# Making the residual stream channel-major in a three-pass encoder-layer kernel

## Chip, cores, metric

The kernel runs as one program on the 8 cores of one Trainium2 chip; each core handles half of one prompt stream and four short sample streams. The metric is device time in microseconds (us) of the slowest core. In some executions the cores of one die show a lower granted TensorE clock and the run is some per cent longer (up to 3032 us here, with 0.81 to 0.82 on one die and 0.985 to 0.986 on the other). Only fast runs are compared below, unless a median of all runs is said to include a slow one.

TensorE is called PE, VectorE DVE, ScalarE ACT, GpSimd POOL, as in the profile.

## The reference, cut to what matters

One layer on 8192 prompt frames x 4 streams and 16 frames x 32 sample streams, D = 1024, feed-forward width 2816 = 22 x 128:

```python
x = x + 0.5 * swiglu_ffn(x, g_ff1, w_ff1_in, w_ff1_out)       # pass A: "first FFN"
z = rms_norm(x, g_mix) @ w_in                                  # pass B: "mixer"
#   conv group: GLU -> depthwise conv (31) -> LayerNorm -> swish
#   attention group: 8 q / 2 kv heads, window of 3 chunks, sinks
x = x + concat([c_out, a_out]) @ w_out                         # "output product"
x = x + 0.5 * swiglu_ffn(x, g_ff2, w_ff2_in, w_ff2_out)       # pass C: "second FFN"

def swiglu_ffn(x, g, w_up, w_down):
    a, b = split(rms_norm(x, g) @ w_up)                        # "up product"
    return (silu(a) * b) @ w_down                              # "down product"
```

All three passes read the residual x from HBM and write it back.

## The kernel before

The cuts of code in this document are shortened: within a function too, lines are left out, and `# [...]` marks a longer gap.

The program records every operation and then orders each engine's instructions with a list scheduler on a cost model; the order is static, so PE takes its matmuls in that order and waits where one isn't ready. That is why nearly every instruction of the profile has one source line; groups are told apart by tile names. Tiles of the first FFN begin with `A_`, of the mixer with `B_`, of the second FFN with `C_`.

x is row-major: 128 frames on the partitions, 1024 channels along the free dimension. A norm then works on one number per partition (0.16 us an operation in the trace), but the up product contracts over channels, so every normed group of 128 rows goes through PE as eight transposes:

```python
def norm_vec(self, x, n, G):                 # x: [128 rows, 1024]
    O.act(out=b[0:n, :], in_=x[0:n, :], func=AF.Square, accum_out=ssq)
    rsqrt(O, ssq, 1.0 / D, v, y, t, u)       # Newton on [128, 1] operands
    O.stt(b[0:n, :], x[0:n, :], y, G[0:n, :], ALU.mult, ALU.mult)

def transposes(self, b, n):
    for k in range(8):
        self.O.tr(p[:, k * 128:k * 128 + n], b[0:n, k * 128:(k + 1) * 128], self.K.IDB[0:n, 0:n])

def up(self, bi, bg):                        # blocks of 384 columns (the first: 448 or 320)
    for j in range(NJ):
        for h, ps in ((0, a), (1, b)):
            for k in range(8):
                O.mm(ps[:, 0:N], W[:, k, h * 128:(h + 1) * 128], X[:, k, 0:N], k == 0, k == 7)
# [...]
def down(self, bi, bg):                      # rows stationary, w_down moving (512 wide)
    for gi, g in enumerate(self.blocks[bi]):
        for h in range(2):
            for j in range(NJ):
                O.mm(p[0:n, :], self.H[:, j, off:off + n], self.WD[:, j, h * 512:(h + 1) * 512], j == 0, j == NJ - 1)
            O.stt(x[0:n, h * 512:(h + 1) * 512], p[0:n, :], 0.5, x[0:n, h * 512:(h + 1) * 512], ALU.mult, ALU.add)
# [...]
def load_x1(self, r, n):                     # mixer: x comes back from HBM, ring of three tiles [128, 1024]
    i = self.nxt("x1", 3)
    self.O.dma("gpsimd", "bx1%d" % i, self.X1[i][0:n, :], self.d.x1[r:r + n, :], rk=[("x1", r)])

def out_pe(self, r, n, lhs, h):              # output product: mixer rows stationary, w_out moving
    for k in range(8):
        O.mm(p[0:n, :], lhs(k), self.WO[:, k, h * 512:(h + 1) * 512], k == 0, k == 7)

def out_post(self, r, n, h):
    self.O.tt(x[0:n, c], self.pb[1 - h][0:n, :], x[0:n, c], ALU.add)
    if h == 1:
        self.O.dma("gpsimd", "bx2%d" % i, self.d.x2[r:r + n, :], x[0:n, :], wk=[("x2", r)])
# [...]
def loads(F):                                # second FFN's weights, loaded while the mixer still runs
    for j in range(NJ):
        F.load_w(j)                          # w_up: 22 tiles, into memory that frees during the mixer
    for j in range(NJ):
        F.load_d(j)                          # w_down: into memory that frees at the mixer's end
```

Of the kernel before, what the change touches and what calls it, by code (L numbers as in the profile page):

```python
# [7 lines left out]
F32 = mybir.dt.float32  # L8
# [9 lines left out]
SLACK = 2  # L18
# [8 lines left out]
class Prog:  # L27
# [124 lines left out]
    def schedule(self, rounds=3):  # L152
# [18 lines left out]
        def run(before, after, prio, back):  # L171
# [24 lines left out]
            for _ in range(n):  # L196
# [9 lines left out]
                if dma[u] and not back:  # L206
                    pipe = max(pipe, end + 0.5) + wire[u]
                    end = max(pipe, end + 1.5) + 0.3 + SLACK
                dirty = {e}
                for x in after[u]:  # L210
                    left[x] -= 1
                    lat = 0.06 if eng[x] == e else 0.16 + (MARGIN if back else 0.0)
                    if back and dma[x]:
                        lat += 2.0 + SLACK + wire[x]
                    if ready[x] < end + lat:
                        ready[x] = end + lat
                    if not left[x]:
                        release(x)
                        dirty.add(eng[x])
# [220 lines left out]
HALO0 = HALF  # L440
SAMP0 = HALF + 128
NROWS = HALF + 192
# [5 lines left out]
def bcast_rows(ap1, n=128):  # L448
    return ap1.partition_broadcast(n)


class FF:
# [3 lines left out]
    def __init__(self, K, carves, tag, wu, wd, g1, g2, blocks, src, dst, xnd=None, rkey=None, wkey=None, nkey=None, low=None, cwd=None, weng="gpsimd", hook=None):  # L456
# [3 lines left out]
        self.rkey, self.wkey, self.nkey = rkey, wkey, nkey  # L460
        nmax = max(sum(n for _, n in b) for b in blocks)
        self.weng, self.hook = weng, hook
        c0, c1, c2 = carves
        self.XA = [c0([128, D], F32, "xa") for _ in range(2)]
        self.XB = [c0([128, D], BF16, "xb") for _ in range(2)]
        self.G1 = c0([128, D], F32, "g1")
        self.SM = c0([128, 8, 16], F32, "sm")
        self.XNT = [c0([128, 8, nmax], BF16, "xnt") for _ in range(2)]
        self.SA = [c0([128, nmax], F32, "sa") for _ in range(2)]
        self.nmax = nmax  # L470
        self.H = c0([128, NJ, nmax], BF16, "h")
        self.H_off = c0.off - (NJ * nmax * 2 + 63) // 64 * 64
# [3 lines left out]
        c3 = c0 if cwd is None else cwd  # L476
        self.WD = c3([128, NJ, 1024], BF16, "wd")
        self.XR = [c3([128, D], F32, "xr") for _ in range(3)]
        self.XO_off = c3.off
        self.XO = [c3([128, 8, 128], BF16, "xo") for _ in range(2)] if g2 is not None else None  # L480
        self.G2 = c3([128, D], F32, "g2") if g2 is not None else None
        self.cnt = dict(xa=0, xr=0, xb=0, xo=0, sm=0, ab=0, d=0, t=0)
        self.g1, self.g2 = g1, g2
# [3 lines left out]
        self.xa, self.xr = {}, {}  # L487

    def nxt(self, k, n):
        i = self.cnt[k]  # L490
        self.cnt[k] += 1
        return i % n

    def load_g(self, which):
        G, g = (self.G1, self.g1) if which == 1 else (self.G2, self.g2)
        if G is not None:
            self.O.dma("sync", self.tag + "g%d" % which, G[:, :], bcast_rows(g))

    def stage(self):

        O, P = self.O, self.K.P
        lo = self.XO_off
        ring = self.XR + [self.G2, P.sbuf(self.tag + "_sx", [128, D], F32, lo)]
        chunks = [(self.WU[j][:, h * 1024:(h + 1) * 1024], self.wu[j][:, h * 1024:(h + 1) * 1024]) for j in range(NJ) for h in range(2)]
        chunks += [(self.WD[:, j, :], self.wd[j]) for j in range(NJ)]
        for i, (dst, src) in enumerate(chunks):
            s = ring[i % len(ring)]
            O.dma("sync", self.tag + "sg%d" % (i % len(ring)), s[:, :], src)
            O.cp(dst, s[:, :])

    def first(self):

        O, P, off = self.O, self.K.P, self.H_off + 22 * self.nmax * 2 - 12288
        xs = self.XA + [P.sbuf(self.tag + "_xh%d" % i, [128, D], F32, off + 4096 * i) for i in range(2)]
        bs = self.XB + [P.sbuf(self.tag + "_bh%d" % i, [128, D], BF16, off + 8192 + 2048 * i) for i in range(2)]
        for i, (r, n) in enumerate(self.blocks[0]):
            O.dma("gpsimd" if i % 2 else "sync", self.tag + "xh%d" % i, xs[i][0:n, :], self.src[r:r + n, :])
        self.load_g(1)
        self.stage()
        sm = self.SM[:, :, :].rearrange("p a b -> p (a b)")  # L520
        O.memset(sm[:, 0:4], 1.0)
        for i, (r, n) in enumerate(self.blocks[0]):
            O.act(out=bs[i][0:n, :], in_=xs[i][0:n, :], func=AF.Square, accum_out=sm[0:n, i:i + 1])
        y = sm[:, 8:12]
        rsqrt(O, sm[:, 0:4], 1.0 / D, sm[:, 4:8], y, sm[:, 12:16], sm[:, 16:20])
        o = 0
        for i, (r, n) in enumerate(self.blocks[0]):
            O.stt(bs[i][0:n, :], xs[i][0:n, :], y[0:n, i:i + 1], self.G1[0:n, :], ALU.mult, ALU.mult)
            p = self.transposes(bs[i], n)
            O.act(out=self.XNT[0][:, :, o:o + n], in_=p, func=AF.Copy)  # L530
            o += n

    def load_w(self, j):
        k = [("pc", self.tag + "u", j)] if self.weng == "sync" else []
        self.O.dma(self.weng, self.tag + "wu%d" % (j % 8), self.WU[j][:, :], self.wu[j], rk=k)

    def load_d(self, j):
        k = [("pc", self.tag + "d", j)] if self.weng == "sync" else []
        self.O.dma(self.weng, self.tag + "wd%d" % (j % 8), self.WD[:, j, :], self.wd[j], rk=k)

    def load_xa(self, g):
        r, n = g
        i = self.nxt("xa", len(self.XA))
        self.xa[g] = self.XA[i]
        self.O.dma("sync", self.tag + "xa%d" % i, self.XA[i][0:n, :], self.src[r:r + n, :], rk=self.rkey(g) if self.rkey else ())

    def load_xr(self, g):
        r, n = g
        i = self.nxt("xr", len(self.XR))
        self.xr[g] = (self.XR[i], i)  # L550
        self.O.dma("sync", self.tag + "xr%d" % i, self.XR[i][0:n, :], self.src[r:r + n, :], rk=self.rkey(g) if self.rkey else ())

    def norm_vec(self, x, n, G):
        O = self.O
        b = self.XB[self.nxt("xb", 2)]
        sm = self.SM[:, self.nxt("sm", 8), :]
        ssq, v, y, t, u = (sm[0:n, i:i + 1] for i in range(5))
        O.act(out=b[0:n, :], in_=x[0:n, :], func=AF.Square, accum_out=ssq)
        rsqrt(O, ssq, 1.0 / D, v, y, t, u)
        O.stt(b[0:n, :], x[0:n, :], y, G[0:n, :], ALU.mult, ALU.mult)  # L560
        return b

    def transposes(self, b, n):
        p = self.PT[self.nxt("t", 2)][:, :].bitcast(BF16)
        with self.O.group():
            for k in range(8):
                self.O.tr(p[:, k * 128:k * 128 + n], b[0:n, k * 128:(k + 1) * 128], self.K.IDB[0:n, 0:n])
        return p.rearrange("p (k n) -> p k n", k=8)[:, :, 0:n]

    def norm1(self, bi):  # L570

        O = self.O
        X = self.XNT[bi % 2]
        off = 0
        prev = None
        for g in self.blocks[bi] + [None]:
            cur = None
            if g is not None:
                cur = (self.norm_vec(self.xa[g], g[1], self.G1), g[1], off)
                off += g[1]  # L580
            yield
            if prev is not None:
                b, n, o = prev
                p = self.transposes(b, n)
                O.act(out=X[:, :, o:o + n], in_=p, func=AF.Copy)
            prev = cur
            yield

    def tail(self, g):

        O = self.O
        (r, n) = g
        x, xi = self.xr[g]
        O.dma("gpsimd", self.tag + "st%d" % xi, self.dst[r:r + n, :], x[0:n, :], wk=self.wkey(g) if self.wkey else ())
        if self.G2 is None:
            return
        b = self.norm_vec(x, n, self.G2)
        yield
        yield
        p = self.transposes(b, n)  # L600
        i = self.nxt("xo", 2)
        O.act(out=self.XO[i][:, :, 0:n], in_=p, func=AF.Copy)
        O.dma("gpsimd", self.tag + "xo%d" % i, self.xnd(g), self.XO[i][:, :, 0:n], wk=self.nkey(g))
        yield

    def up(self, bi, bg):
        O = self.O
        N = sum(n for _, n in self.blocks[bi])
        X = self.XNT[bi % 2]
        for j in range(NJ):  # L610
# [13 lines left out]
            if j == 10:  # L624
                assert not self.pend
                for g in self.blocks[bi][0:3]:
                    self.load_xr(g)

    def run(self, prologue=None):
        self.pend = []  # L630
        norm = [None]

        def bg(k):
            for _ in range(k):
                while self.pend:
                    try:
                        next(self.pend[0])
                        return
                    except StopIteration:
                        self.pend.pop(0)  # L640
# [1005 lines left out]
```

## Time and profile before

2573 us, the median of four runs (one of them slow, at 2976; the mean of the three fast ones is 2572.8). The profiled run is a fast one; the slowest of its cores spans 2569.6 us.

I cut the span at PE events that can be read off the trace of each core, and take the median of the eight cores:

| stage | from / to | before, us | PE idle in it |
|---|---|---|---|
| start-up | start / end of the first down product | 148.4 | |
| first FFN | / its last down matmul | 883.8 | 0.6 |
| mixer | / the last output matmul | 598.7 | 53.5 |
| gap | / the second FFN's first down matmul | 34.1 | 11.2 |
| second FFN | / its last down matmul | 889.5 | |
| tail | / end | 9.2 | |

The mixer and the gap aren't mixer work alone: the up product of the second FFN's first block is woven into them.

The page of the kernel before: busy time of the engines, the busy tenths of PE and its granted clock in 40 slices of the span, and the chain of work that ended last.

```profile
PE 2463.4 (96%) x14740; PEld 1354.3 (53%) x14740; DVE 1063.0 (41%) x2748; ACT 748.8 (29%) x1307; POOL 202.4 (8%) x356
...
PE   6999999999999999899899969799999999999998
...
PEclk9999999999999999899999979999999999999999
...
PE 91%; DMA 4%; DVE 2%; issue 2%; ACT 1%; DVEq 0%; SPq 0%; POOL 0%; POOLq 0%; ACTq 0%
```

PE is the kernel's chain nearly everywhere. Slices 24 and 26 (about 1478 to 1540 and 1606 to 1670 us) are not full.

Windows of the same core: the stretch and its length, the busy time of PE, PEld (weight loads), DVE, ACT and POOL with instruction counts, then PE's granted clock, DMA's busy share, and GB/s.

```profile
300.00:364.00 64.00, 64.00 (x384) 35.35 (x383) 31.62 (x101) 18.53 (x31) 8.61 (x14) 1.00 0.42 117
1478.00:1542.00 64.00, 39.84 (x242) 22.86 (x242) 41.51 (x99) 33.79 (x48) 14.06 (x23) 0.76 0.84 261
1542.00:1606.00 64.00, 63.25 (x407) 38.23 (x405) 32.23 (x88) 17.63 (x30) 13.95 (x25) 1.00 0.71 231
1606.00:1670.00 64.00, 46.15 (x253) 24.59 (x250) 20.33 (x61) 10.39 (x18) 6.20 (x12) 0.90 0.77 251
1800.00:1864.00 64.00, 64.00 (x362) 34.90 (x360) 14.83 (x33) 9.32 (x18) 1.06 (x2) 1.00 0.12 38
```

In the steady FFN windows PE is busy 64 of 64 us and DVE less than half: what PE is given to do there is the time. At the mixer's end PE is idle for 24 of 64 and 18 of 64 us, with DMA at 0.84 and 0.77.

### The profile page before, as it was taken

To read this page: it belongs to the slowest core of one execution; us is meant where nothing else is said; L and a number is where in the kernel's file an instruction comes from. 1 tells how busy PE (TensorE), PEld (TensorE's weight loads), DVE (VectorE), ACT (ScalarE), POOL (GpSimd) and SP (SyncE) were. 2 spreads that over 40 slices of the span, in tenths; PEclk is the share of its full clock that TensorE was granted. 3 is DMA by queue.
4 is the path that set the end of the run, shared out by engine and by line. 5 is a ranking of instruction groups with operands and counts; after the bars stand their busy time and mean duration, and the time that the engine had idled before them with its cause. 6 is when DMAs were issued, how large, how long until landed. Compare 5 with 4: busy or idle time off the path is not lost.

```text
span 2569.6 us, 41607 instructions; the slowest of 8 cores (2559.8 to 2569.6 us)
## 1 busy us (share of the span) xinstructions
PE 2463.4 (96%) x14740; PEld 1354.3 (53%) x14740; DVE 1063.0 (41%) x2748; ACT 748.8 (29%) x1307; POOL 202.4 (8%) x356
## 2 busy tenths in 40 slices
PE   6999999999999999899899969799999999999998
PEld 3355555555556555455455535355555555555554
DVE  5454344335434432564876865321233223313211
ACT  3122232223213211465766652111121112112210
POOL 0011011011101000010111122000000000000000
PEclk9999999999999999899999979999999999999999
DMA  9965344344434433433355787721112111210110
GB/s 277 306 180 116 76 112 121 74 93 123 108 75 108 111 101 101 108 88 94 93 148 165 208 261 232 250 70 50 34 49 74 50 42 58 74 49 27 40 50 25
DMA packets 116867, 284.24 MB, mean 111 GB/s; under 512 B 33983, under 2 KB 51391, under 8 KB 115703
## 3 DMA queue, kind: packets, MB, share of 16 engines
q1 hardware_dynamic: 86359, 166.28, 21.8%
q0 software_dynamic: 30304, 115.29, 16.2%
q8 instruction: 121, 1.98, 0.3%
q14 instruction: 83, 0.68, 0.1%
HBM read 230.89 MB, written 97.86 MB: 128 GB/s over the span
## 4 chain that ended last, share of the span: by engine, by line
PE 91%; DMA 4%; DVE 2%; issue 2%; ACT 1%; DVEq 0%; SPq 0%; POOL 0%; POOLq 0%; ACTq 0%
PE PS L373 91%; DMA A_xr<-wu 1%; DMA C_xa<-x 1%; DMA B_x_159<-x 1%; ACT B_pt L373 0%; DMA A_xa<-xin 0%; DVE C_sm L373 0%; DMA A_xr<-wd 0%; DVE B_y L373 0%; DMA C_wu<-wu2b 0%; DMA B_x_158<-x 0%; DVE A_wu L373 0%; DVE A_xb L373 0%; DVE A_sm L373 0%; DVE B_x_158 L373 0%
## 5 line engine op out<-in xcount | busy, mean ns | idle before, releaser
L373 PE MATMUL PS<-A_xnt,A_wu 128*128 128x384 bf16 (+1 forms) x3872 | 652.7, 329 | 8.5 <-DVE A_wu L373 6.6
L373 PE MATMUL PS<-C_xnt,C_wu 128*128 128x384 bf16 (+1 forms) x3872 | 632.4, 325 | 7.3 <-DMA C_wu<-wu2b 6.4
L373 PEld LDWEIGHTS PS<-A_xnt,A_wu 128*128 128x128 bf16 x3872 | 376.1, 98 | 267.5 <-issue 17.4
L373 PEld LDWEIGHTS PS<-C_xnt,C_wu 128*128 128x128 bf16 x3872 | 379.8, 98 | 251.2 <-issue 8.3
L373 ACT ACTIVATE C_sa<-PS 128x384 f32<-128x384 f32 (+1 forms) x242 | 117.4, 485 | 759.0 <-PE PS L373 718.5
L373 PE MATMUL PS<-A_wd,A_h 128*128 128x512 bf16 x1496 | 331.1, 379 | 0.7 <-DVE A_h L373 0.7
L373 PE MATMUL PS<-C_wd,C_h 128*128 128x512 bf16 (+1 forms) x1452 | 317.3, 381 | 0.0
L373 DVE TENSOR_TENSOR C_h<-PS,C_sa 128x384 bf16<-128x384 f32 (+1 forms) x242 | 133.2, 551 | 374.5 <-PE PS L373 369.2
L373 DVE TENSOR_TENSOR A_h<-PS,A_sa 128x384 bf16<-128x384 f32 (+1 forms) x242 | 135.9, 562 | 285.5 <-PE PS L373 282.4
L373 PEld LDWEIGHTS PS<-A_wd,A_h 128*128 128x128 bf16 x1496 | 142.8, 98 | 182.0 <-issue 19.1
L373 ACT ACTIVATE A_sa<-PS 128x384 f32<-128x384 f32 (+1 forms) x242 | 119.7, 495 | 408.0 <-PE PS L373 337.3
L373 PEld LDWEIGHTS PS<-C_wd,C_h 128*128 128x128 bf16 (+1 forms) x1452 | 143.1, 99 | 171.2 <-issue 3.1
L373 DVE SCALAR_TENSOR_TENSOR C_xr<-PS,C_xr 128x512 f32<-128x512 f32 (+1 forms) x66 | 45.6, 691 | 273.9 <-PE PS L373 273.9
L373 PE MATMUL PS<-B_xn,B_wi 128*128 128x512 bf16 x512 | 119.8, 380 | 1.5 <-DVE S_ux L373 1.5
L373 DVE SCALAR_TENSOR_TENSOR A_xr<-PS,A_xr 128x512 f32<-128x512 f32 (+1 forms) x68 | 46.5, 689 | 150.6 <-PE PS L373 150.5
L373 PE MATMUL PS<-B_wi,B_xn 128*128 128x256 bf16 (+1 forms) x512 | 98.8, 346 | 5.1 <-ACT B_pt L373 5.1
L373 ACT ACTIVATE A_xb<-A_xr 128x1024 bf16<-128x1024 f32 (+1 forms) x34 | 35.8, 1054 | 224.7 <-DVE A_xr L373 223.3
L417 POOL DMA_DIRECT2D yout<-C_xr x33 | 17.6, 534 | 906.7 <-DVE C_xr L373 906.7
L373 PEld LDWEIGHTS PS<-B_wi,B_xn 128*128 128x128 bf16 x512 | 51.0, 102 | 45.3 <-issue 14.7
L373 PEld LDWEIGHTS PS<-B_xn,B_wi 128*128 128x128 bf16 x512 | 47.4, 98 | 51.8 <-issue 4.3
L373 DVE SCALAR_TENSOR_TENSOR A_sm<-A_sm 128x1 f32<-128x1 f32 (+2 forms) x390 | 61.0, 158 | 31.2 <-DVE A_sm L373 1.8
L373 ACT ACTIVATE B_pt<-PS 128x1024 bf16<-128x1024 f32 (+2 forms) x68 | 65.9, 982 | 24.5 <-PE PS L373 24.4
(192 smaller groups left out, 2028.0 us busy)
## 6 DMA issues: line engine op xcount, KB each, us to landing
A_xr<-xin SPq DMA_DIRECT2D x33, 512.0 KB, 3.7
x<-A_xr POOLq DMA_DIRECT2D x33, 512.0 KB, 3.1
C_xa<-x SPq DMA_DIRECT2D x32, 512.0 KB, 3.8
C_xr<-x SPq DMA_DIRECT2D x32, 512.0 KB, 3.7
yout<-C_xr POOLq DMA_DIRECT2D x32, 512.0 KB, 2.9
B_wr<-wdc SPq DMA_DIRECT2D x28, 576.0 KB, 4.6
A_xa<-xin SPq DMA_DIRECT2D x31, 512.0 KB, 5.4
A_xr<-wu SPq DMA_DIRECT2D x27, 512.0 KB, 7.9
```

The source lines that it names most:

```text
L373: o = self.P.add(eng, lambda e: getattr(e, meth)(**kw), r, w, cost=self.cost(eng, meth, kw))
L417: self.P.add(eng, lambda e: e.dma_start(out=out, in_=in_), r, w, lane=lane, rk=rk, wk=wk, cost=1.0 if eng == "gpsimd" else 0.5, nbytes=n * ...
```

## The change

The intent: hold x with channels on the partitions ([128, 8, columns]) in all three passes, so that no normed row has to be transposed. What that takes:

- the sum of squares now runs over partitions: ACT squares each of the 8 channel slices, DVE adds them, and PE multiplies the sum (split in two bf16 parts) by a matrix of 1/1024, which gives every partition the mean: two matmuls per norm ("ones-products");
- the inverse root is computed on [128, columns] instead of [128, 1];
- down and output products turn round: weights stationary, columns moving. FFN blocks become 432 columns (first FFN, ten blocks) and 416 (second FFN), instead of eleven of 384 (the first of them 448 or 320);
- the mixer reads the residual in half tiles ([128, 512], a ring of four) and the conv output through three buffers instead of one; the copies that reordered it go, since a strided moving operand does the same;
- the first FFN loads x once instead of twice, and start-up uses eleven staging slots instead of five;
- the scheduler's backward pass charges a DMA's time on a shared pipe, not on each edge.

The core of the diff, with cuts marked (the lines under "blocks" are parts of longer calls):

```diff
@@ scheduler, backward pass
+                elif dma[u]:
+                    pipe = max(pipe, t) + wire[u]
+                    end = max(pipe, t) + cost[u]
...
-                        lat += 2.0 + SLACK + wire[x]
+                        lat += 2.0 + SLACK
@@ class FF
-    def transposes(self, b, n):
-        with self.O.group():
-            for k in range(8):
-                self.O.tr(p[:, k * 128:k * 128 + n], b[0:n, k * 128:(k + 1) * 128], self.K.IDB[0:n, 0:n])
+    def square(self, X, c, n):
+        O.act(out=sq[:, 0:n], in_=X[:, c, 0:n], func=AF.Square)
+        ...
+            O.tt(S, S, sq[:, 0:n], ALU.add)
+    def rstd(self, n, act=False):
+        O.cp(hi, S)
+        O.tt(lo, S, hi, ALU.subtract)
+        with O.group():
+            O.mm(p, self.K.ONEB[:, :], hi, True, False)
+            O.mm(p, self.K.ONEB[:, :], lo, False, True)
+        ...
+        rsqrt(O, p, self.V[:, 0:n], self.Y[:, 0:n], self.T[:, 0:n], S)
+    def apply1(self, bi):
+        for c in range(8):
+            self.O.stt(self.XNT[:, c, 0:n], X[:, c, 0:n], self.G1[:, c:c + 1], self.Y[:, 0:n], ALU.mult, ALU.mult)
@@ down
-                        O.mm(p[0:n, :], self.H[:, j, off:off + n], self.WD[:, j, h * 512:(h + 1) * 512], j == 0, j == NJ - 1)
+                    O.mm(p[:, 0:n], self.WD[:, j, c * 128:(c + 1) * 128], self.H[:, j, 0:n], j == 0, j == NJ - 1)
@@ memory of the second FFN
         self.WU += [c2([128, 2048], BF16, "wu") for j in range(fits, NJ)][::-1]
+        self.X.append(c3([128, 8, nmax], F32, "x"))
         self.WD = c3([128, NJ, 1024], BF16, "wd")
@@ class Mixer
-        self.X1 = [C([128, D], F32, "x1") for _ in range(3)]
+        self.X1 = [C([128, 512], F32, "x1") for _ in range(4)]
-                O.mm(p[0:n, :], lhs(k), self.WO[:, k, h * 512:(h + 1) * 512], k == 0, k == 7)
+                mv = mc[:, 4 * k:4 * k + 4, :] if k < 4 else ma[:, k - 4, :, :].rearrange("p g (a s i) -> p s (g a) i", a=2, s=4)
+                O.mm(p, self.WO[:, k, c * 128:(c + 1) * 128], mv, k == 0, k == 7)
@@ blocks
-    [main[0:2] + [halo, samp]] + b3          # first FFN: 448 columns, then 10 x 384
+    cut(0, NCOLS, 432)                       # 9 x 432 and 400
-    [main[0:2] + [samp]] + b3                # second FFN: 320 columns, then 10 x 384
+    cut(SAMP0, NCOLS, 416)                   # 10 x 416
```

The first block of the second FFN, whose up product is woven into the mixer, grows from 320 to 416 columns.

## The prediction

> **What bounds it now.** By the page's busy table PE is 96% of 2569.6 us and 91% of the chain that ended last. The timeline splits it: first FFN to 1033, mixer 1033 to about 1640 (with the second FFN's first block woven in), second FFN's steady part from 1670. In the windows of both steady FFN parts PE is busy 64 of 64 us at clock 1.00. There a 384-column matmul follows the last every 162.5 ns (20 more take 3.25 us), a 512-column one 215.9 ns (110 in 23.9 us), eight transposes 0.45 us.[...] Losses outside: start-up (first block's down product ends at 149.9 us; about 105 us of PE work), and the mixer's end (PE 40 of 64 and 46 of 64 us in two windows, clock 0.76 and 0.90, DMA share 0.77 to 0.84).
>
> **What the change does to PE's work.**
> - Removed: 808 transposes, 101 x 0.45 = 45 us.
> - Added: two ones-products per norm, 30 norms x 2 x 0.18 = 11 us.
> - Down product with weights stationary and columns moving: the 64-row group no longer pays for 128 rows, -4.75 us per FFN.
> - Up: 10 blocks of 432/416 instead of 11 of 384:[...]
> Sum about -44 us, nearly all where PE is the whole chain.
>
> By block: first FFN 88.4 us per 384 columns becomes an estimated 97.1 per 432 (64.2 up, 32.1 down, 0.7 ones); ten later blocks 884 us become eight of 97.1 and a last one of 90.0, 867. Second FFN after its first up product: 899 becomes 870.
>
> **Start-up.** DMA-bound at 277 to 306 GB/s. x is loaded once, not twice, the two broadcast gains go: about 2.5 MB less before the last weight. Eleven staging slots replace five, and half of w_down is cast by the DMA. I expect the first down product to end at 132 to 145 us, not 149.9: about -10 (its 16 fewer columns are paid in the 867).
>
> **Mixer.** Same number of output products; the copies that reorder conv output (0.42 us each) go; conv output is read through three buffers instead of one. The strided moving operand is free: projections that read so already run 8 in 1.9 us, like contiguous ones. Against: residual ring of four half tiles instead of three whole, twice the DMA issues on POOL (0.55 us each),[...] and 14 us more up product in the first block of the second FFN, which falls into the gap. Net about 0, plus or minus 15.
>
> **VectorE.** Norm work becomes wide (26 operations of about 0.58 us for the two inverse roots of a block alone): an estimated 51 of 97 us per block. Not binding.
>
> **Sum:** -17 -10 -29 +0 = -56: 2518 us; 8 in 10: 2493 to 2546. Faster by over 2%: 0.57; within 2%: 0.41; slower: 0.02.
>
> **Checks.** No transposes of normed rows; PE gap 182.5 ns at 432 columns; PE busy 64 of 64 in steady windows; first FFN ends near 1005; second FFN after its first up product 870 us; first down ends by 145.
>
> **What would make it wrong.** The static order mis-timing the long norm chain, so that PE waits in order for ones-products; a half-tile residual ring that starves the output products at the mixer's end under weight loading (+20); or, the other way, the gap at the mixer's end closing (-30).

Where a cut is marked, the record had a formula for the spacing of matmuls, two terms in the sum of PE's work that rested on that formula (together -0.6 us), and the size of reads in the list for the mixer. The recorded sum of "about -44 us" has the two cut terms in it; the terms that stand come to -45 + 11 - 9.5 = -43.5 us. The forecast of -56 us is added up from the stages and the cut terms are not added there; its FFN stages were worked out with the cut formula. Estimated from the kernel before alone they come out the same: the line through its 162.5 ns at 384 columns and 215.9 at 512 gives 169.2 at 400, 175.8 at 416 and 182.5 at 432. For the 64-row group, the trace of the kernel before has matmuls of 512 columns 216.5 ns apart with 64 rows stationary (40 in 8.66 us), and 215.9 with 128; 44 of them take 9.5 us, and half of that is the 4.75. The 0.58 us of a wide DVE operation is the author's estimate; the kernel before shows 0.556 us for 384 columns and 0.619 for 448 (bf16 out, f32 in).

## More of the kernel before

PE's timeline in the gap of the kernel before (start, duration, operation, and in brackets the idle time ahead of it and what ended it):

```profile
1634.37 1.03 PE L373 MATMUL PS<-B_wo,B_ma 128*128 128x512 bf16 x4
1641.78 21.55 PE L373 MATMUL PS<-C_xnt,C_wu 128*128 128x320 bf16 x128 [6.38 <-DMA C_wu<-wu2b]
...
1669.77 1.01 PE L373 MATMUL PS<-K_t,C_xb 128*128 128x128 bf16 x8 [5.55 <-DVE C_sm L373]
1670.58 4.78 PE L373 MATMUL PS<-C_wd,C_h 128*128 128x512 bf16 x12
```

The last output matmul ends at 1635.4; then PE waits for late tiles of w_up, has 128 up matmuls of its first two blocks left, waits for a norm, and starts the down product.

## The result

The changed kernel takes 2539.2 us (median of four runs, 2535.3 to 2615.2; the 2615 is slow: one die at clock 0.95). Ratio to the kernel before 0.9864, 95% interval 0.9842 to 0.9887. Ratios are the mean time of one kernel's fast runs over that of the other's of the same rounds, so not quite the ratio of the medians. That is 34 us gained (35 by the means of the fast runs) where 55 were predicted, inside the predicted range; it is within 2%, to which the prediction had given a chance of 0.41, and 0.57 to more.

| stage (median of 8 cores, us) | before | after | measured | predicted |
|---|---|---|---|---|
| start-up | 148.4 | 141.5 | -6.9 | -10 |
| first FFN | 883.8 | 869.2 | -14.6 | -17 |
| mixer | 598.7 | 611.1 | +12.4 | mixer and gap together: |
| gap | 34.1 | 36.6 | +2.5 | 0, give or take 15 |
| second FFN and tail | 898.7 | 869.7 | -29.0 | -29 |

Medians of stages don't add up exactly; the median end of a core moves by -34.4, that of the slowest core by -33.4. So start-up and the two FFNs came within about 3 us each, and mixer and gap together missed by 15 us, the edge of the range that the prediction gave for them.

The page of the changed kernel, the same lines as above:

```profile
PE 2408.4 (95%) x13908; PEld 1301.6 (51%) x13908; DVE 1205.7 (48%) x2261; ACT 661.0 (26%) x1205; POOL 298.9 (12%) x499
...
PE   4999999999999999999999869699999999999998
...
PEclk9999999999999999999999989899999999999999
...
PE 88%; DMA 4%; DVE 3%; issue 2%; ACT 1%; SPq 1%; DVEq 0%; POOLq 0%; ACTq 0%
```

PE's busy time fell by 55 us, the span of the slowest core by 33: PE sat idle 106 us before (2569.6 - 2463.4) and 128 after (2536.2 - 2408.4). Windows of the changed kernel (columns as above; the third is 77 us long and holds the gap):

```profile
300.00:364.00 64.00, 64.00 (x353) 34.32 (x351) 36.29 (x64) 9.98 (x19) 5.95 (x9) 1.00 0.20 53
1455.00:1519.00 64.00, 45.79 (x302) 25.14 (x300) 37.90 (x75) 34.47 (x57) 15.45 (x27) 0.89 0.72 233
1519.00:1583.00 64.00, 61.90 (x324) 32.04 (x325) 22.18 (x38) 12.30 (x20) 24.77 (x43) 0.97 0.61 196
1583.00:1660.00 77.00, 50.42 (x238) 23.20 (x237) 30.04 (x51) 8.18 (x17) 14.00 (x26) 0.83 0.60 188
1800.00:1864.00 64.00, 64.00 (x366) 35.61 (x364) 22.57 (x41) 9.27 (x18) 1.43 (x2) 1.00 0.06 21
```

The steady windows are full again, and DVE, with all its wide norm work, is at 36 of 64 us (an estimated 55 of a block's 97.1, where 51 were predicted): not binding there, as predicted. PE's timeline in one steady block shows what was removed and added; first the kernel before, then the changed one:

```profile
319.74 0.61 PE L373 MATMUL PS<-K_t,A_xb 128*128 128x128 bf16 x8
320.18 9.66 PE L373 MATMUL PS<-A_wd,A_h 128*128 128x512 bf16 x44
```

```profile
309.54 0.53 PE L376 MATMUL PS<-A_sh,K_t 128*128 128x432 bf16 x2
309.91 32.28 PE L376 MATMUL PS<-A_h,A_wd 128*128 128x432 bf16 x176
342.03 4.54 PE L376 MATMUL PS<-A_xnt,A_wu 128*128 128x432 bf16 x24
...
407.00 5.27 PE L376 MATMUL PS<-A_h,A_wd 128*128 128x432 bf16 x28
```

By starts (the duration of a line runs to the modelled end of its last matmul, past the start of the next line): eight transposes took 320.18 - 319.74 = 0.44 us; two ones-products take 0.37; 176 down matmuls of 432 columns take 342.03 - 309.91 = 32.12 us, 182.5 ns each; a whole block takes 407.00 - 309.91 = 97.1 us. All four are what the prediction had.

The gap of the changed kernel, on PE:

```profile
1629.11 1.03 PE L376 MATMUL PS<-B_ma,B_wo 128*128 128x512 bf16 x4
1643.65 0.50 PE L376 MATMUL PS<-C_sh,K_t 128*128 128x416 bf16 x1 [13.51 <-DVE C_sh L376]
1644.34 0.51 PE L376 MATMUL PS<-C_sh,K_t 128*128 128x416 bf16 x1 [0.19 <-DVE C_sh L376]
1653.79 12.79 PE L376 MATMUL PS<-C_xnt,C_wu 128*128 128x416 bf16 x48 [8.94 <-DVE C_xnt L376]
1666.41 13.88 PE L376 MATMUL PS<-C_h,C_wd 128*128 128x416 bf16 x78
```

Where the kernel before had 128 up matmuls here, there are 48, and 23 us of idle time instead of 11. PE waits for block 1's ones-product, whose x is loaded only after the mixer's memory is free, then for the rest of the norm. Meanwhile the queue engine SP issues w_down (its timeline in the gap):

```profile
1629.78 1.65 SPq L420 DMA_DIRECT2D C_wd<-wd2b  x3
1631.48 2.21 SPq L420 DMA_DIRECT2D C_x<-x  x3
1633.78 24.96 SPq L420 DMA_DIRECT2D C_wd<-wd2b  x19
```

The last w_down load is issued at 1658.7; by the trace it lands at 1661.6, 5 us before the first down matmul. Both chains, w_down's load and block 1's norm, start when the mixer ends, and they finish nearly together.

And the chain of waits of the changed kernel, in order of time, from just before the first up matmul of the second FFN to the norm in the gap:

```profile
1520.05 0.70 DVE B_x_156 L376
1521.10 98.13 PE PS L376 x512
1619.90 0.69 DVE B_x_156 L376
...
1632.26 7.14 DMA C_x<-x
```

98 us of PE work without a break lie between the first up product and nearly the last output product. That line is the main reading of this study: in this stretch there is no idle time into which more up product could fall.

### The profile page after: what moved, and what is told of

It is laid out like the page before. It is cut to its first block, busy times and chain, and to the rows that moved or that the text cites. A ratio compares the mean times of both kernels' runs of the same rounds, so it can differ in the third digit from the quotient of the medians.

```text
span 2536.2 us, 38840 instructions; the slowest of 8 cores (2523.7 to 2536.2 us)
## 1 busy us (share of the span) xinstructions
PE 2408.4 (95%) x13908; PEld 1301.6 (51%) x13908; DVE 1205.7 (48%) x2261; ACT 661.0 (26%) x1205; POOL 298.9 (12%) x499
## 4 chain that ended last, share of the span: by engine, by line
PE 88%; DMA 4%; DVE 3%; issue 2%; ACT 1%; SPq 1%; DVEq 0%; POOLq 0%; ACTq 0%
PE PS L376 88%; DMA A_x<-xin 2%; DMA A_st_86<-wu 1%; DMA B_wr<-wdc 1%; DMA A_st_95<-wd 1%; SPq L420 1%; DVE B_y L376 0%; ACT B_se L376 0%; ACT B_pt L376 0%; DMA C_x<-x 0%; DVE A_xnt L376 0%; DMA zd<-B_z 0%; DVE C_u L376 0%; DVE B_z L376 0%; DVE B_t_109 L376 0%
## 5 line engine op out<-in xcount | busy, mean ns | idle before, releaser
L376 PE MATMUL PS<-A_xnt,A_wu 128*128 128x432 bf16 (+1 forms) x3520 | 647.3, 346 | 16.4 <-DVE A_xnt L376 7.3
L376 PE MATMUL PS<-C_xnt,C_wu 128*128 128x416 bf16 x3520 | 627.3, 340 | 9.3 <-DVE C_xnt L376 8.9
L376 DVE TENSOR_TENSOR C_h<-PS,C_sa 128x416 bf16<-128x416 f32 x220 | 130.0, 591 | 448.5 <-PE PS L376 428.2
L376 PE MATMUL PS<-A_h,A_wd 128*128 128x432 bf16 (+1 forms) x1760 | 322.5, 346 | 3.8 <-DVE A_wd L376 3.3
L376 PE MATMUL PS<-C_h,C_wd 128*128 128x416 bf16 x1760 | 311.1, 339 | 0.0
L376 ACT ACTIVATE C_sa<-PS 128x416 f32<-128x416 f32 x220 | 113.9, 518 | 609.3 <-PE PS L376 603.6
L376 PEld LDWEIGHTS PS<-A_h,A_wd 128*128 128x128 bf16 x1760 | 172.6, 98 | 151.9 <-issue 6.4
L376 DVE TENSOR_TENSOR A_h<-PS,A_sa 128x432 bf16<-128x432 f32 (+1 forms) x220 | 132.5, 603 | 247.1 <-PE PS L376 224.2
L376 PEld LDWEIGHTS PS<-C_h,C_wd 128*128 128x128 bf16 x1760 | 172.2, 98 | 137.3
L376 ACT ACTIVATE A_sa<-PS 128x432 f32<-128x432 f32 (+1 forms) x220 | 115.8, 527 | 436.5 <-PE PS L376 404.4
L376 DVE SCALAR_TENSOR_TENSOR C_x<-PS,C_x 128x416 f32<-128x416 f32 x80 | 47.2, 590 | 164.1 <-PE PS L376 164.1
L376 PEld LDWEIGHTS PS<-B_xn,B_wi 128*128 128x128 bf16 x512 | 47.2, 98 | 55.1 <-issue 5.5
```

What stands on the lines that cost most here:

```text
L376: o = self.P.add(eng, lambda e: getattr(e, meth)(**kw), r, w, cost=self.cost(eng, meth, kw))
```

## The experiments

The diffs are shortened, and some lines joined. Times of experiments are the means of their fast runs; ratios, with 95% intervals, are to the kernel before in the same rounds. "Traces" below are the profiled runs' stage medians over eight cores, with the names of the table; M+gap is mixer and gap together. The quoted texts use letters for theories; each says in its own words what they mean in that run. My main theory after the result was: the added up product in the mixer (first block 320 to 416 columns: 352 matmuls x 40 ns = 14 us, an estimate from the traces' 135.8 ns a matmul at 320 columns, 72 in 9.78 us before, and 175.8 at 416, 304 in 53.45 us after) is paid in full. Rivals: the half-tile residual ring and its traffic starve the output products; or the late loads in the gap cost it.

Splitting the traces at the first up matmul of the second FFN puts the idle time where it belongs:

| PE idle, us (length of the stretch) | before | after |
|---|---|---|
| last down of first FFN to first up of second | 48.5 (495.1) | 47.2 (504.6) |
| first up to last output product | 4.9 (103.7) | 3.7 (106.1) |
| gap | 11.2 (34.1) | 23.0 (36.6) |

In M+gap the kernel before does 60.4 us of second-FFN work at full speed (400 up matmuls, 48 of them 384 wide, are 55.6; eleven groups of eight transposes at 0.44 are 4.8) and the changed one 71.0 us (400 up matmuls are 70.3, two pairs of ones-products 0.7): 10.6 more. Without it, M+gap is 572.4 us before (632.8 - 60.4) and 576.7 after (647.7 - 71.0). So by arithmetic about 11 of the 15 us, net of all else, are this extra work, and 4 are not explained; the experiments test it.

The net hides three things that the traces show. Of the 15 us, PE is busy for 5.6 (568.7 us of M+gap before, 574.3 after) and idle for 9, all of the added idle time in the gap: part of the cost shows as work, part as an emptier gap. The middle stretch itself grew by only 2.4 us, though its up product grew from 272 matmuls to 352 wider ones (25 us more): 72 output matmuls now run ahead of it, in a stretch that grew by 9.5. And PE's waits in the mixer changed hands (medians of eight cores): for block 0's norm 17.5 us before and 0.6 after, for the residual adds of the output products 6.3 before and 20.8 after.

### e1_first320: the first block small again

```diff
-    cut(SAMP0, NCOLS, 416)
+    [(SAMP0, 320)] + cut(SAMP0 + 320, NCOLS, 384)
```

> Second FFN's first block cut back to 320 columns (ten blocks of 384 after it), everything else as changed. Theory A (up product woven into the mixer's end is paid in full): first-FFN end to last output product shrinks from about 611 by 10 to 14 us, the second FFN after its first down product start grows by about 15, total within 3 us of the changed kernel. Theory B (the half-tile residual ring leaves holes there that the up product fills for free): the mixer's stretch stays within 4 us of 611, total 10 to 17 us slower than the changed kernel.

Measured: 2542.4 us, ratio to before 0.9871 (0.9814 to 0.9929). Traces: M+gap 637.4 instead of 647.7, so 10.3 of the 14 us came back (8.7 of them in the mixer, where theory A wanted 10 to 14); the second FFN took 877.2 instead of 861.0, since more, narrower blocks follow. The total didn't improve. Put otherwise, 16 of the 29 us that the second FFN gained in the changed kernel are work that was only moved into the mixer. This supports "paid in full" for about seven tenths; it isn't exactly what either theory gave. It also shows that the small first block isn't the cure: the columns have to be done somewhere where PE is the chain.

### e2_noresload and b1_noresload: no residual reload in the mixer (wrong results on purpose)

The mixer doesn't load x and doesn't add it: e2 in the changed kernel, b1 in the kernel before.

```diff
-        self.O.dma("gpsimd", "bx1%d" % i, self.X1[i][:, :], self.d.x1[:, c, c0:c0 + 512], rk=units("x1", c0, 512))
-        self.O.tt(xv, self.pb[1 - c % 2].rearrange("p (s b i) -> p s b i", s=4, i=16), xv, ALU.add)
+        self.O.ts(xv, self.pb[1 - c % 2].rearrange("p (s b i) -> p s b i", s=4, i=16), 1.0, None, ALU.mult)
```

> Mixer's output products written without adding the residual: no loads of the residual stream in the mixer (wrong result on purpose). Theory B (residual ring starves the output products): PE's waits on the residual adds (20 us in the changed kernel) vanish and the mixer's stretch shrinks by 12 to 20 us. Theory A: it shrinks by less than 6 us, though 16 MB of reads are gone.

> The kernel BEFORE, without loading and adding the residual in the mixer (wrong result on purpose), the twin of the same cut in the changed kernel, which took 32 us from the stretch between the first FFN's end and the second FFN's first down product (up work counted off). If the half-tile ring is what costs (theory B), the cut takes at most 15 us here. If the residual stream costs the mixer about the same in both kernels (theory A, whole tiles or half tiles do not matter), it takes 25 us or more here too.

Measured: e2 2503.7 us, ratio 0.9721 (0.9675 to 0.9768); b1 2540.2 us, 0.9818 (0.9742 to 0.9893). Traces: M+gap falls by 32.2 us in the changed kernel (to 615.5) and by 29.6 in the kernel before (to 603.2). That the reload would be worth so much in the changed kernel was a miss of my expectation. PE's waits on the residual adds, which theory B wanted gone, fell only from 20.8 to 15.4 us in e2, so most of them aren't waits for the loads. And the reload is worth nearly the same in both: the mixer as a whole is slowed by its residual traffic, and the new form of that traffic is not what makes the difference between the two kernels. One run alone, e2, would have led to the wrong verdict; its twin on the kernel before decided it.

### e6_ring6: six half tiles in the ring

```diff
-        self.MC = [C([128, 16, 128], BF16, "mc") for _ in range(3)]
-        self.X1 = [C([128, 512], F32, "x1") for _ in range(4)]
+        self.MC = [C([128, 16, 128], BF16, "mc") for _ in range(2)]
+        self.X1 = [C([128, 512], F32, "x1") for _ in range(6)]
```

> Six half tiles in the residual ring instead of four, paid for with one of the three conv-output buffers. Theory B: PE's waits on the residual adds (20 us) fall by more than half and the stretch (648 us) by 10 us or more. Theory A: within 5 us.

Measured: 2533.2 us, ratio 0.979 (0.9714 to 0.9867). The kernel before was noisy in this job, 2573 to 2600 us in its fast runs, so this ratio is not to be set beside those of other jobs. Traces: M+gap 645.9 instead of 647.7. The total is 5 us under the changed kernel's, but only 2 of them are in mixer and gap. Depth of the ring, as far as it can be told from the conv-output buffer given up for it, doesn't explain 15 us. Idle between first up and last output product went from 3.7 to 0, but there was nothing more to gain there.

### e4_lanes: w_down over eight semaphores instead of three

w_down's loads take turns on three semaphores, so a fourth waits for the first to land. This spreads them over eight.

```diff
-        self.O.dma(self.weng, "Fsg%d" % (8 + j % 3), self.WD[:, j, :], ...)
+        self.O.dma(self.weng, "bwi%d" % (j % 8), self.WD[:, j, :], ...)
```

> w_down of the second FFN loaded over eight semaphores instead of three, so eight loads may be in flight and a load no longer waits for the third before it. Theory C (the 36 us between last output product and first down product are the serial load of w_down): the gap falls to 18 to 28 us and the whole by 8 to 18 us. If the loads are limited by memory that frees late or by bandwidth, the gap stays above 32.

Measured: 2535.6 us, ratio 0.9845 (0.9792 to 0.9898). Traces: the gap is halved, 36.6 to 17.9 us, and yet the end comes only 2 us earlier, where 8 to 18 were expected. PE in the gap of e4:

```profile
1656.34 0.50 PE L376 MATMUL PS<-C_sh,K_t 128*128 128x416 bf16 x1 [16.93 <-DVE C_sh L376]
...
1657.33 9.66 PE L376 MATMUL PS<-C_h,C_wd 128*128 128x416 bf16 x44
1670.28 9.93 PE L376 MATMUL PS<-C_h,C_wd 128*128 128x416 bf16 x46 [3.29 <-DVE C_x L376]
```

The down product now starts at once after the ones-product, with the order changed so that the 48 up matmuls of block 1, which used to fill part of the gap, come after it (the second FFN takes 876.4 instead of 861.0). PE's wait for block 1's ones-product itself stays, and grew to 16.9. A limit behind the limit: two chains that begin at the same event have to be moved together.

### e7_layout: w_down early, w_up late

w_down moves into the memory that frees early and late w_up tiles take its place (with e4's semaphores).

```diff
-        self.WU += [c2([128, 2048], BF16, "wu") for j in range(fits, NJ)][::-1]
         self.X.append(c3([128, 8, nmax], F32, "x"))
-        self.WD = c3([128, NJ, 1024], BF16, "wd")
+        self.WU += [c1([128, 2048], BF16, "wu") for j in range(fits, NJ)]
+        self.WD = c2([128, NJ, 1024], BF16, "wd")      # for the second FFN
```

> w_down placed in the memory that frees when the convolution ends, 13 tiles of w_up instead in the memory that frees at the mixer's end; eight semaphores for w_down. Theory C: w_down is loaded before the mixer ends, up product follows the last output product within about 5 us while its tiles arrive; stretch plus gap together (648 us) fall by 15 to 30 us. If bandwidth at the mixer's end is the limit rather than where w_down sits, they fall by less than 8 us.

Measured: 2538.5 us, ratio 0.9856 (0.9809 to 0.9903). Traces: M+gap 643.3, a fall of 4 us where theory C wanted 15 to 30; the end at 2532.1 is 3 us later than in the changed kernel. The number is that of the rival in the quoted text (bandwidth), but the trace shows another reason. The gap's idle time fell to 5.5 us, but 208 of the 352 up matmuls of block 0 moved out of the mixer into the gap, and the mixer's idle time rose from 50.8 to 68.3. In the gap of e7 PE now has up product to do (one line of its timeline):

```profile
1618.64 39.20 PE L376 MATMUL PS<-C_xnt,C_wu 128*128 128x416 bf16 x208 [5.50 <-DMA C_wu<-wu2b]
```

The work was the filler between output products; taken from there, it leaves a hole there: after the first up product PE waits 18 us for residual adds, where the changed kernel waits 4. Idle time was moved, not removed.

### e9_early: block 1's x early, three late w_up tiles

```diff
+        late = 0 if low is None else 3
+        if late: self.X.append(c2([128, 8, nmax], F32, "x"))       # memory that frees with the convolution
-        self.WU += [c2([128, 2048], BF16, "wu") for j in range(fits, NJ)][::-1]
+        self.WU += [c2([128, 2048], BF16, "wu") for j in range(fits, NJ - late)][::-1]
         self.WD = c3([128, NJ, 1024], BF16, "wd")
+        self.WU += [c3([128, 2048], BF16, "wu") for j in range(late)]
```

with e4's semaphores, and with the first down product of the second FFN taken tile by tile into all eight of the kernel's PSUM buffers as w_down lands.

> Second FFN: block 1's x placed in memory that frees when the convolution ends (it displaces three late tiles of w_up), w_down over eight semaphores with its early-freed tiles first, and the first down product taken tile by tile as w_down arrives (as the first FFN's is). Theory C' (the gap's 23 us of idle PE are the serial norm chain of block 1 and the load of w_down, both starting only when the mixer's memory frees): idle in the gap falls below 10 us, and total falls by 12 to 22 us against the changed kernel, to 2517 to 2527. If not, total within 6 us of it.

Measured: 2532.4 us, fast runs 2525.8 to 2543.9, ratio 0.9766 (0.9663 to 0.9869, the noisy job). Traces: idle in the gap falls from 23.0 to 9.1, the end comes 4 us earlier than in the changed kernel (by the means of the fast runs, from another job, 5.5). The waits for block 1's norm are gone; PE now waits for the late w_up tiles, which still lie in memory that frees at the mixer's end:

```profile
1648.21 8.14 PE L376 MATMUL PS<-C_xnt,C_wu 128*128 128x416 bf16 x32 [5.04 <-DMA C_wu<-wu2b]
1659.15 4.66 PE L376 MATMUL PS<-C_xnt,C_wu 128*128 128x416 bf16 x16 [2.81 <-DMA C_wu<-wu2b]
```

The direction was right, the size a miss.

### e5_sched and b2_sched: the scheduler's backward pass alone

e5 puts the old backward pass into the changed kernel; b2 puts the new one into the kernel before.

```diff
-                elif dma[u]:
-                    pipe = max(pipe, t) + wire[u]
-                    end = max(pipe, t) + cost[u]
-                        lat += 2.0 + SLACK
+                        lat += 2.0 + SLACK + wire[x]
```

> Only the change to the static scheduler's backward pass is undone. If the order of instructions is not where the expected gain went, total within 8 us of the changed kernel (2539); if that part of the change was worth something, 8 to 30 us slower, nearly all of it in the mixer's stretch and the gap.

> The kernel BEFORE with only the scheduler's changed backward pass. If that part of the change is worth by itself what undoing it cost in the changed kernel (about 10 us, all in the mixer), this is 5 to 12 us faster than the kernel before. If it only pays together with the new layout, within 4 us of the kernel before.

Measured: e5 2548.4 us (fast runs 2547.9 to 2549.0), ratio 0.9849 (0.9773 to 0.9925, the noisy job). Traces: mixer 621.3 instead of 611.1, everything else within 3 us. The total is 8 us above that of after2 (below), the changed kernel on the same chip. So without these lines of the change the mixer would have lost 10 us more. b2: 2574.2 us, ratio to before 0.9991 (0.9974 to 1.0009): worth nothing by itself. This part of the change, which I had not costed at all, pays only together with the new layout. It also means that the remainder of the mixer (572.4 and 576.7 us above) is nearly equal only net: something in the new mixer costs about 10 us under the old order, and the new order gives it back. What that is was not tested.

### after2, e11_tiles, e12_tiles_ring6: all limits of the gap moved together

e11 joins what e4, e7 and e9 had shown one by one: w_down as 22 separate tiles, so that each can lie where memory frees and be loaded alone; block 1's x where the convolution's memory frees; the three late w_up tiles in attention-output buffers that free four output blocks before the end; eight semaphores; the first down product tile by tile.

```diff
-        self.WD = c3([128, NJ, 1024], BF16, "wd")
+            self.X.append(c2([128, 8, nmax], F32, "x"))
+            self.WU += [c2([128, 2048], BF16, "wu") for j in range(fits, NJ - 3)][::-1]
+            a = [c3([128, 1024], BF16, "wd") for j in range(13)]
+            c3.off = ma2                                   # attention output, blocks 2 and 3 of the ring
+            self.WU += [c3([128, 2048], BF16, "wu") for j in range(3)]
+            b = [c3([128, 1024], BF16, "wd") for j in range(2)]
+            self.WD = b + a + [c3([128, 1024], BF16, "wd") for j in range(7)]
-            self.down(bi, bi == 0 and prologue is None)
+            self.down(bi, bi == 0)                         # tile by tile in the second FFN too
```

e12 is e11 with e6's ring. after2 is the changed kernel again, on the same chip and in the same rounds.

> The changed kernel unaltered, so that the next two stand beside it on the same chip and in the same rounds. 2530 to 2545 us; from the first FFN's last down product to the second FFN's first down product about 648 us (611 + 37), with about 23 us of TensorE idle in the last 37.

> The changed kernel with four things moved together at the end of the mixer: w_down of the second FFN in 22 separate tiles, block 1's x in memory that frees when the convolution ends, the three last w_up tiles in attention-output buffers that free four output blocks early, and the first down product taken tile by tile as w_down lands. Theory A (the 37 us after the last output product are bounded by w_down's load and block 1's norm chain, both started late): all 400 up products are done by the last output product, the stretch shrinks to 8 us or less with under 5 us idle in it, and the whole kernel is 8 to 18 us under the changed kernel of the same rounds. Rival (the idle is paid anyway, by another wait just behind, as when the lanes were widened): within 6 us of the changed kernel.

> The run before with the residual ring of six half tiles instead of four (one conv-output buffer fewer). Theory A (the ring does not bind): within 5 us of the run before. Theory B (the half-tile ring starves the output products): 8 us or more faster than it.

Measured (all results correct):

| kernel | fast runs, us (mean) | ratio to before (95%) | M+gap | idle in gap | second FFN |
|---|---|---|---|---|---|
| after2 | 2537.4 to 2543.7 (2540.3) | 0.9858 (0.9841 to 0.9874) | 647.0 | 22.7 | 861.0 |
| e11_tiles | 2522.0 to 2527.2 (2524.4) | 0.9796 (0.9781 to 0.9812) | 620.4 | 0.0 | 874.2 |
| e12_tiles_ring6 | 2515.6 to 2520.9 (2518.5) | 0.9773 (0.9756 to 0.9791) | 618.2 | 0.0 | 870.0 |

e11 is 15.8 us under the changed kernel (means of the fast runs), within the 8 to 18 expected. Theory A wanted all 400 up matmuls done by the last output product; the 352 of block 0 are, the 48 of block 1 aren't. M+gap fell by 27 us, of which 13 went to the second FFN: 8.4 for the 48 up matmuls of block 1 that now come after the first down product, and the rest is mostly a wait of the down product, which takes all eight of the kernel's PSUM buffers, for the last output products to be added from theirs (5.6 us on the slowest core):

```profile
1645.88 31.86 PE L376 MATMUL PS<-C_h,C_wd 128*128 128x416 bf16 x172 [5.56 <-DVE B_x L376]
```

e12 takes 6.0 us more off by the means of the fast runs, 5.4 by their medians: just over what I had called "the ring does not bind", and short of the 8 for "it starves". With the gap closed, the deeper ring is worth more than it was in e6; the wait ahead of the down product is gone. PE at the end of e12's mixer:

```profile
1638.53 0.69 PE L376 MATMUL PS<-C_h,C_wd 128*128 128x416 bf16 x3
1639.60 30.58 PE L376 MATMUL PS<-C_h,C_wd 128*128 128x416 bf16 x173 [0.39 <-DVE C_h L376]
```

Three lines of e12's chain of waits say it shortly: from the second FFN's first up product on, 108 us of PE work without a break, 0.6 us of DVE, and on into the down product.

```profile
1530.90 107.81 PE PS L376 x563
1638.87 0.60 DVE C_h L376
1639.60 40.42 PE PS L376 x229
```

e12 beats both kernels: 2.3% under the kernel before, where the change alone had 1.4%.

## Why the prediction was right, and where it wasn't

**Start-up, -10: measured -7.** The down product ends at 141.5 instead of 148.4 (145.0 in after2, the same kernel). Right within its range (132 to 145).

**First FFN, -17: measured -14.6; second FFN, -29: measured -29.0.** The terms that can be read off the trace were as predicted: 97.1 us a block, 182.5 ns for a matmul of 432 columns, 0.37 us for a pair of ones-products, no transposes of normed rows. The argument was sound because PE is busy 64 of 64 us there, with no idle time to hide in. The estimate rested on the spacing of matmuls at the new width. The line through what the kernel before shows, 162.5 ns at 384 columns and 215.9 at 512, gives 182.5 at 432, and 182.5 was measured. Of the 2.4 us missing in the first FFN, 1.7 are PE idle time; what it waits for there was not looked into.

**Mixer, "14 us more up product in the first block of the second FFN, which falls into the gap. Net about 0": measured +15,** at the edge of the "plus or minus 15" beside it. This is the step that failed, and the word that failed is "falls into the gap". I had seen idle time in two windows of the mixer's end and counted it as room for the 14 us. It was not room for them. Of the 64 us of idle in mixer and gap before, 48 lie ahead of the first up product, when block 0's norm isn't there yet; 11 lie in the gap; 5 are between. The up product stands in the middle stretch, where PE is the chain (98 us unbroken). The idle time of the gap waits for loads and a norm that start only when the mixer's memory frees, and its length hardly depends on what PE has to do: 34.1 us with 128 up matmuls in it, 36.6 with 48. So the change added 10.6 us of work where it costs in full (14 of up product and 0.7 of ones-products, less the transposes that went). It left up product out of the gap, where it had cost nothing, and the gap stayed as long and stood emptier: 23.0 us of idle instead of 11.2. What is shown for this: the two splits of the traces, e1 (10 of 14 us come back with the small block), e7 (taking 208 up matmuls out of the mixer opens 17.5 us of idle time there), and e11 and e12 (with loads and norm moved ahead, the gap's idle time goes to zero and the kernel gains 16 us, and 22 with the deeper ring). About 4 of the 15 us are not traced to anything.

Could it instead have been the half-tile ring, which the prediction named as a risk (+20)? Not the most of it: reload traffic costs the mixer about 30 us in both kernels (32.2 in e2, 29.6 in b1), and a deeper ring gives 2 us alone (e6) and 6 once the gap is closed (e12). Nor is it the strided moving operand of the output product: where PE is at full clock, a matmul of 512 columns follows the last every 216 ns in both kernels. The other cost that the prediction named, more DMA issues on POOL (0.56 to 0.58 us each for the residual in the changed kernel), was not tested apart.

**The named risk "PE waits in order for ones-products"** did happen, once: 13.5 us in the gap, and 8.9 for the norm behind it. It costs little by itself, since w_down lands hardly earlier, but it is the reason why loading w_down faster gained almost nothing (e4). "VectorE not binding" was right in throughput and left out latency: the root is now a chain of twelve dependent operations on 416 columns, from 1644.96 to 1652.87 us, 7.9 us, plus eight applies of 0.57 us, where before a group's chain ran on single columns at 0.16 us an operation.

**What I had left out.** PE also ran at a lower clock after its idle stretch in the gap. There the windows of the changed kernel show (PE alone: length, busy, clock, DMA share, GB/s):

```profile
1654.00:1658.00 4.00, 3.60 (x8) 0.50 0.87 241
1658.00:1662.00 4.00, 4.00 (x16) 0.65 0.60 184
1662.00:1666.00 4.00, 4.00 (x25) 1.00 0.00 0
```

The 48 up matmuls after the wait took 12.8 us, where 48 at 175.8 ns are 8.4. By their starts in the trace, the first eight take 4.2 us (to 1658.03), the next eight 346 ns each (to 1660.79), the rest 175.8. So of the 4.2 us lost, an estimated 2.7 are the clock (16 at 346 instead of 175.8) and 1.5 waits of the first eight for the applies. The trace shows a clock of 0.50 when work began again, and full spacing 7.0 us later (1653.79 to 1660.79), the first 4.2 of them with waits between matmuls. The scheduler's part of the change, worth 10 us in the changed kernel's mixer (e5), I had not costed either. That the total fell inside the predicted range, which ends at 2546, owes to it, and so to luck: without it the changed kernel takes 2548.4 us.

**What stays open.** The 48 us of PE idle ahead of the first up product are the largest hole left. They shrink when the reload traffic goes (to 35.4 in e2, 41.3 in b1), but no correct version was tried. Also open: what in the new mixer costs the 10 us that the scheduler's change gives back; what the longer waits for residual adds (20.8 us instead of 6.3) would be worth if the norm of block 0 came earlier; and about 7 of the 27 us that e12 took out of the gap (22.7 idle, 4.2 slow matmuls), since mixer, gap and second FFN together fell by 20. About 4 of them show as a longer stretch ahead of the first up product (504.0 to 507.9 us); the rest I did not follow.

## What to carry to other kernels

Idle time on the bounding engine is room for more work only if that work can run at that time: before you say that added work "falls into a gap", find the gap in the trace, ask what ends it, and ask whether the added work's inputs are there and its place in the engine's order is in the gap. When several chains begin at the same event (here: memory that frees when a stage ends), speeding up one of them shows little (e4: the end came 2 us earlier); move all of them ahead of the event, for instance by cutting one big tile into many that fit where memory frees earlier. And where a deletion looks like it proves a cost, delete the same thing from the kernel before as well: only a difference between the two explains the difference between the kernels.
